# A hybrid decoder layer: how the plain weight tiles are split into high and low parts

## The chip, the cores and the metric

The kernel runs on one core of one Trainium2 chip. The metric is the device time of one execution in microseconds; of before there are three runs. The profile is of one execution of the same program, taken by the hardware profiler.

## The reference

One decoder layer works on 528 tokens (16 learned ones, then 512) of width 1024, float32:

```
h += 1/2 SwiGLU(rmsnorm(h))                 # 1024 -> 2 x 2816 -> 1024
u  = rmsnorm(h) @ w_in                      # q, k, v, forget gate, retention q, k, v, g, two gates
a  = forgetting attention, 16 heads of 64, causal, with a bias from the running log forget gate
b  = retention, 4 heads (128 -> 256), in chunks of 128, group norm, swish gate
h += (g_a * (a @ w_o_fox) + g_b * (b @ w_o_ret)) @ w_out
h += 1/2 SwiGLU(rmsnorm(h))
```

The result must agree with float32. So every float32 operand of a dense product is split: a high part that TensorE's float32r format holds exactly, and a low part, the operand less the high part. A product is three passes: high x high, high x low, low x high.

## The kernel before

Features lie on the 128 partitions, tokens on the free axis. A weight matrix is cut into *pieces* of 128 output features: 8 blocks of 128 x 128 beside each other (1024 columns), or for the output tiles of a SwiGLU 6 or 5 blocks (768 or 640 columns). The program takes the pieces in one fixed order, which is TensorE's own order, written out by hand; the list `SEQ` gives it for a SwiGLU. `n`, `a`, `b` are whole hidden tiles, `e` and `l` are hidden tiles made with seven products of quarters instead of eight, `p` is an output tile. After the first SwiGLU come the projections (`proj`, with the attention woven between them), the retention, three square products of eight output tiles each (`oa`, `ob`, `ow`), and the second SwiGLU. TensorE's instructions keep the program's order. For the other engines and the DMA queues a planner chooses the order: it takes what is ready by its own estimate of times, within the order of the program's priorities, so it also moves transfers ahead of older work once a buffer is free. Each queue then runs strictly in the order chosen.

There are two kinds of weight tiles. An *S* tile (kind `"S"`, 14 in each SwiGLU) serves an `e`/`l` pair; sums of its quarters are made by VectorE (`wsums`), and quarters and sums are split. All other tiles are *plain* (kind `"w"`). `load` brings a tile of 2048 columns (two pieces) on SP's queue into one of two float32 buffers (tag `w`); an S tile has two buffers of its own. `ready` makes the pieces `wh` and `wl` (tags of that name, four buffers each) by `split`: ScalarE copies the source into `wh`, VectorE subtracts `wh` from the source into `wl`. `weights()` hands TensorE's next piece over and calls `ready` for three pieces, that one and the next two. The first two pieces come from the tile `w0`, which is loaded in four quarters between the loads of the eight chunks of `h`; they are split in halves, alternating with `gained`, which makes the operands `n1uh` and `n1ul` from `h`. ScalarE and VectorE keep the program's order only in this first stage.

GpSimd's own work is small: constants at the start, some of which wait for the vector tile `VEC`; for each of 16 heads the load of a bias row `B` (line 760) and a sum `Bd` (line 761); the reloads of the gates `gs` (line 1034) and of `hh` (line 1091).

In the profile the copies into `wh` stand at line 105, the subtractions into `wl` at line 106, the tile loads at line 178, the matmuls of a whole piece at line 277. TensorE's groups are named by what they write: `fpa`, `fpb` (hidden tiles of the first SwiGLU), `fq` (its quarter products), `fpo` (its output tiles), `spa`, `spb`, `sq`, `spo` (the same of the second).

Of the kernel before, what the change touches and what calls it, by code (L numbers as in the profile page):

```python
"""Hybrid decoder layer (FoX attention + retention between two half SwiGLU blocks), one core.

Everything is kept feature-major: features on partitions, tokens on the free axis.  The zero rows
that the reference puts before the meta tokens are masked everywhere, so the token axis here has the
16 meta tokens followed by the 512 main ones.  Dense products split both float32 operands exactly
into a float32r high and low part and take three passes (hh, hl, lh).  Most hidden tiles of the
SwiGLU blocks are computed by seven products of quarters (output halves x contraction halves x token
halves) instead of eight; the sums of quarters are float32 sums, split exactly like the other operands.
"""
# [22 lines left out]
# The order of a SwiGLU's work on the tensor engine, one token a piece or two of weights:  n0, n1: the  # L32
# first two hidden tiles; aj, bj: the halves of hidden tile j; ej, lj: a hidden tile by seven products of
# quarters, its first four and its last three; pi: the next output tile of the i-th part of the hidden
# tiles.  ui marks where the i-th chunk's sums of quarters are made.
# [17 lines left out]
# Tensor engine work (in units of its time) put between the steps of the attention: FOXFILL scales it,  # L53
# CREDIT is the number of the gates' tiles that go with a pair of heads.
# [10 lines left out]
def layer(tc, order, hT, wf1i, wf1o, wf2i, wf2o, wmix, wsq, vecs, cs, rmask, rvec, cmask, outT):  # L65
# [3 lines left out]
    with ExitStack() as es:  # L69
# [24 lines left out]
        def po_(a):  # L94
            """Where token 0 lies in a two-bank PSUM tile: no matmul's tokens cross the banks."""
            return PO if a == 0 else PM
# [15 lines left out]
        def weave(main, fill):  # L112
            """Emit main; what it yields is the tensor engine time to fill before it goes on."""
            have = 0.0
            for need in main:
                have -= need
                while have < 0:
                    got = next(fill, None)
                    if got is None:
                        have = 0.0  # L120
                        break
                    have += got

        # ---------------------------------------------------------------- the weights' stream
# [43 lines left out]
        def load(n):  # L168
            while at["l"] < min(n, len(loads)):
                i = at["l"]  # L170
                src, w, kind = loads[i]
                if kind == "S":
                    if st["sp"] is None:
                        return
                    raw[i] = st["sp"].tile([128, 2048], F32, name=f"w{i}", tag="wS", bufs=2)
                else:
                    raw[i] = wp.tile([128, 2048], F32, name=f"w{i}", tag="w", bufs=2)
                ld = nc.sync.dma_start(raw[i][:, :w], src[:, :w])
                if i == 5:
                    with tc.issue_after(ld.ins):  # L180
                        nc.sync.dma_start(RV, rvec)
                at["l"] += 1

        def wsums(i):
            """Sums of a weight tile's quarters A11, A12, A21, A22: S1, S2, S4, and S3 in A21's place."""
# [9 lines left out]
        def ready(n):  # L195
            while at["p"] < min(n, len(pieces)):
# [7 lines left out]
                wh = wp.tile([128, 1024], F32R, name=f"wh{i}", tag="wh", bufs=4)  # L204
                wl = wp.tile([128, 1024], F32R, name=f"wl{i}", tag="wl", bufs=4)
                got[i] = wh, wl
                at["p"] += 1
                if i < 2:
                    for x in (0, 512):
                        split(wh[:, x:x + 512], wl[:, x:x + 512], raw[li][:, c + x:c + x + 512])  # L210
# [5 lines left out]
                else:  # L216
                    split(wh[:, :w], wl[:, :w], raw[li][:, c:c + w])

        def weights():
            i = at["u"]  # L220
            at["u"] += 1
            ready(i + 3)
# [3 lines left out]
        # ---------------------------------------------------------------- constants and first loads  # L226
# [4 lines left out]
        w0 = wp.tile([128, 2048], F32, name="w0", tag="w", bufs=2)  # L231
        raw[0] = w0
        at["l"] = 1
        for k in range(KC):
            if k < 4:
                nc.sync.dma_start(w0[:, 512 * k:512 * k + 512], wf1i[0][:, 512 * k:512 * k + 512])
# [7 lines left out]
        RV = cp.tile([128, 16], F32, name="RV")  # L244
        zeta, xi, xi2 = RV[:, 0:4], RV[:, 4:8], RV[:, 8:12]
# [22 lines left out]
        # ---------------------------------------------------------------- helpers  # L268
        def mm3(outs, w, x, nk, first=True, last=True):
            """outs = w^T x over nk chunks of 128, three float32r passes; outs: (psum, first token, end)."""  # L270
# [18 lines left out]
        def gained(k, g, u, a, name):  # L289
            """u = h * gain, split into high and low parts."""  # L290
# [14 lines left out]
        def rstd(acc, R, outs, a, name, er=None):  # L305
            """R = rsqrt(mean square + eps) of every token, on all partitions."""
# [16 lines left out]
        # ---------------------------------------------------------------- SwiGLU  # L323
# [4 lines left out]
        def usums(c, gain, a, xs, name):  # L328
            """Sums of the quarters of h * gain * R (chunk halves x token halves), split: they pair
            tokens, which have one scale only when they are normed."""  # L330
# [18 lines left out]
        def ffn(seq, u, gain, a, pst, pq, norm, done, name):  # L349
# [5 lines left out]
            def prod(out, w, off, x, k0, ts, first, last):  # L355
                """out (+)= w^T x over four chunks: one of the seven products of quarters."""
# [864 lines left out]
```

## Time and profile before

| | |
|---|---|
| runs, us | 1394.8 median, 1394.41 to 1395.88 |
| span of the profiled execution, us | 1392.1 |
| whole time of the profiled execution | not given on the page |
| instructions | 22206 |
| bytes moved by DMA | 139.41 MB |

The span runs from the first to the last instruction; what a run takes more lies around it. The page gives each engine's busy time, the chain of work that ended last, the waits with what ended them, and for DMA the share of the core's 16 DMA engines' time. PE is TensorE, ACT ScalarE, DVE VectorE, POOL GpSimd; SPq and POOLq are the queues on which SP and GpSimd issue transfers.

### The profile page before, as it was taken

The page shows a single profiled execution, that of the slowest core. Times are in us where ns is not written, and L with a number is a line of the kernel's source. Part 1 is how long each engine was busy: PE and PEld are TensorE (multiplying, and loading weights), DVE is VectorE, ACT ScalarE, POOL GpSimd, SP SyncE. Part 2 cuts the span into 40 slices and gives each one's busy share as a digit, 9 for nine tenths or more (in the row PEclk, how much of TensorE's full clock was granted, in tenths as well). Part 3 has the DMA queues.
Part 4 walks back from the last instruction along what each step waited for, and adds up shares of the span by engine and source line. Part 5 has one row for each costly group of instructions (what it writes and reads, how often), then busy time and mean ns, then how long its engine had stood idle before and what let it go on. Part 6 is the DMA issues. An engine that isn't in the chain of part 4 may idle for free.

```text
span 1392.1 us, 22206 instructions
## 1 busy us (share of the span) xinstructions
PE 1376.5 (99%) x8871; PEld 1232.8 (89%) x8871; DVE 1007.9 (72%) x1948; ACT 666.7 (48%) x1131; POOL 52.6 (4%) x80
## 2 busy tenths in 40 slices
PE   8999999999999999999999999999999999999999
PEld 7999999999988788877878998888888889899897
DVE  7977877866687676677755866754666977788773
ACT  7433333333567577666754534453435433344331
POOL 0000000000013000010000000000100000000000
PEclk9999999999999999999999999999999999999999
DMA  7123222221513222222222112433521232223302
GB/s 276 46 106 110 79 101 106 84 103 64 201 61 109 92 84 71 90 92 84 92 84 91 61 61 71 139 124 136 191 108 57 80 127 82 99 93 121 109 21 97
DMA packets 27814, 139.41 MB, mean 100 GB/s; under 512 B 3632, under 2 KB 4016, under 8 KB 16576
## 3 DMA queue, kind: packets, MB, share of 16 engines
q1 hardware_dynamic: 24336, 127.31, 25.5%
q0 software_dynamic: 3232, 10.65, 2.6%
q8 instruction: 70, 1.15, 0.3%
q14 instruction: 32, 0.26, 0.1%
q10 hardware_dynamic: 144, 0.04, 0.0%
HBM read 129.56 MB, written 8.42 MB: 99 GB/s over the span
## 4 chain that ended last, share of the span: by engine, by line
PE 96%; DVE 2%; ACT 1%; DMA 0%; issue 0%; SPq 0%; DVEq 0%; ACTq 0%
PE fq L287 10%; PE sq L287 10%; PE fpo L277 9%; PE spo L277 9%; PE pg L277 6%; PE prv L277 3%; PE fpb L277 3%; PE pq L277 3%; PE fpa L277 3%; PE pv L277 3%; PE ow L277 3%; PE spa L277 3%; PE ob L277 3%; PE spb L277 3%; PE prg L277 3%; PE oa L277 3%
## 5 line engine op out<-in xcount | busy, mean ns | idle before, releaser
L105 ACT ACTIVATE wh<-w 128x512 fp32r<-128x512 f32 (+3 forms) x299 | 249.7, 835 | 465.6 <-PE fpo L277 69.1
L106 DVE TENSOR_TENSOR wl<-w,wh 128x512 fp32r<-128x512 f32 (+3 forms) x299 | 282.9, 946 | 68.3 <-ACT wh L105 66.0
L277 PE MATMUL fpo<-fgh,wh 128*128 128x272 f32 x352 | 71.4, 284 | 0.0
L277 PE MATMUL fpo<-fgl,wh 128*128 128x272 f32 x352 | 71.4, 284 | 0.0
L277 PE MATMUL fpo<-fgh,wl 128*128 128x272 f32 x352 | 71.2, 284 | 0.0
L277 PE MATMUL spo<-sgh,wl 128*128 128x512 f32 (+1 forms) x181 | 70.1, 387 | 0.0
L277 PE MATMUL spo<-sgh,wh 128*128 128x512 f32 (+1 forms) x181 | 70.0, 386 | 0.0
L277 PE MATMUL spo<-sgl,wh 128*128 128x512 f32 (+1 forms) x181 | 69.9, 386 | 0.0
L106 DVE TENSOR_TENSOR pl<-PT,ph 128x512 fp32r<-128x512 f32 (+4 forms) x80 | 34.6, 434 | 32.7 <-ACT ph L105 31.5
L106 DVE TENSOR_TENSOR wl<-ws,wh 128x512 fp32r<-128x512 f32 x84 | 57.6, 686 | 0.0
L277 PE MATMUL pg<-n2uh,wh 128*128 128x512 f32 x128 | 56.4, 440 | 0.0
L1116 DVE SCALAR_TENSOR_TENSOR hh<-spo,hh 128x512 f32<-128x512 f32 (+1 forms) x33 | 22.3, 675 | 44.9 <-PE spo L277 44.9
L793 ACT ACTIVATE P<-P,st 128x144 f32<-128x144 f32 (+1 forms) x64 | 36.5, 570 | 36.9 <-DVE st L789 36.1
L277 PEld LDWEIGHTS fpo<-fgh,wl 128*128 128x128 f32 x352 | 54.1, 189 | 0.0
L277 PEld LDWEIGHTS fpo<-fgh,wh 128*128 128x128 f32 x352 | 54.0, 188 | 0.0
L277 PEld LDWEIGHTS fpo<-fgl,wh 128*128 128x128 f32 x352 | 54.0, 188 | 0.0
L105 ACT ACTIVATE wh<-ws 128x512 fp32r<-128x512 f32 x84 | 51.7, 616 | 0.0
L277 PE MATMUL pg<-n2uh,wl 128*128 128x512 f32 x128 | 50.6, 395 | 0.0
L277 PE MATMUL pg<-n2ul,wh 128*128 128x512 f32 x128 | 50.4, 394 | 0.0
L492 DVE SCALAR_TENSOR_TENSOR h<-fpo,h 128x528 f32<-128x528 f32 x32 | 22.6, 707 | 37.8 <-PE fpo L277 37.8
L287 PE MATMUL fq<-n1ul,wh 128*128 128x264 f32 x168 | 48.0, 285 | 0.0
L287 PE MATMUL fq<-n1uh,wh 128*128 128x264 f32 x168 | 47.9, 285 | 0.0
(926 smaller groups left out, 4296.4 us busy)
## 6 DMA issues: line engine op xcount, KB each, us to landing
w<-in_wmix SPq DMA_DIRECT2D x32, 1024.0 KB, 4.9
w<-in_wf2i SPq DMA_DIRECT2D x22, 1024.0 KB, 4.9
w<-in_wf1i SPq DMA_DIRECT2D x21, 1024.0 KB, 4.9
w<-in_wsq SPq DMA_DIRECT2D x12, 1024.0 KB, 4.9
w<-in_wf1o SPq DMA_DIRECT2D x8, 768.0 KB, 4.2
w<-in_wf2o SPq DMA_DIRECT2D x8, 768.0 KB, 4.2
w<-in_wf1o SPq DMA_DIRECT2D x8, 640.0 KB, 3.9
w<-in_wf2o SPq DMA_DIRECT2D x8, 640.0 KB, 3.9
```

What stands on the lines that cost most here:

```text
L105: nc.scalar.activation(xh, src, AF.Copy)
L106: nc.vector.tensor_tensor(xl, src, f32(xh), ALU.subtract)
L277: nc.tensor.matmul(out, p[:, o:o + 128], q[:, a:b], start=first and k == 0 and i == 0, stop=last and k == nk - 1 and i == 2)
L287: nc.tensor.matmul(out, p, q, start=start and i == 0, stop=stop and i == 2)
L492: nc.vector.scalar_tensor_tensor(h[m][:, x:y], ps, 0.5, h[m][:, x:y], ALU.mult, ALU.add)
L793: last["exp"] = nc.scalar.activation(P[i][:, :w], P[i][:, :w], AF.Exp, scale=-1.0, bias=st[:, 2:3], accum_out=sm[:, 0:1])
L1116: nc.vector.scalar_tensor_tensor(h[m][:, x:y], ps, 0.5, h[m][:, x:y], ALU.mult, ALU.add)
```

## The change

The plain tiles have no float32 copy in SBUF any more. Per piece GpSimd issues a transfer that casts the weight from HBM into `wh` (float32r); ScalarE writes minus `wh` into `wl`; and GpSimd issues a second transfer from HBM, which adds the weight to what stands in `wl`. `load` only notes the address of a plain tile. The two float32 buffers' space goes to `wh` and `wl`, six buffers each; `weights()` calls `ready` for five pieces. The first tile `w0` keeps its float32 form, in two buffers of the tag `wl`. The small load of `RV` is issued after the first loads. S tiles, sums, matmuls and their order stay. (The diff also takes out comments.)

```diff
@@ load @@
                 src, w, kind = loads[i]
-                if kind == "S":
-                    if st["sp"] is None:
-                        return
-                    raw[i] = st["sp"].tile([128, 2048], F32, name=f"w{i}", tag="wS", bufs=2)
-                else:
-                    raw[i] = wp.tile([128, 2048], F32, name=f"w{i}", tag="w", bufs=2)
-                ld = nc.sync.dma_start(raw[i][:, :w], src[:, :w])
-                if i == 5:
-                    with tc.issue_after(ld.ins):
-                        nc.sync.dma_start(RV, rvec)
                 at["l"] += 1
+                if kind == "w":
+                    raw[i] = src
+                    continue
+                if st["sp"] is None:
+                    at["l"] -= 1
+                    return
+                raw[i] = st["sp"].tile([128, 2048], F32, name=f"w{i}", tag="wS", bufs=2)
+                nc.sync.dma_start(raw[i], src)
@@ ready @@
-                wh = wp.tile([128, 1024], F32R, name=f"wh{i}", tag="wh", bufs=4)
-                wl = wp.tile([128, 1024], F32R, name=f"wl{i}", tag="wl", bufs=4)
+                wh = wp.tile([128, 1024], F32R, name=f"wh{i}", tag="wh", bufs=6)
+                wl = wp.tile([128, 1024], F32R, name=f"wl{i}", tag="wl", bufs=6)
...
                 if i < 2:
                     for x in (0, 512):
-                        split(wh[:, x:x + 512], wl[:, x:x + 512], raw[li][:, c + x:c + x + 512])
+                        split(wh[:, x:x + 512], wl[:, x:x + 512], raw[li][i][:, x:x + 512])
...
                 else:
-                    split(wh[:, :w], wl[:, :w], raw[li][:, c:c + w])
+
+                    nc.gpsimd.dma_start(wh[:, :w], raw[li][:, c:c + w])
+                    nc.scalar.activation(wl[:, :w], f32(wh[:, :w]), AF.Copy, scale=-1.0)
+                    nc.gpsimd.dma_start(wl[:, :w], raw[li][:, c:c + w], accum_op=ALU.add)
@@ weights @@
-            ready(i + 3)
+            ready(i + 5)
@@ first loads @@
-        w0 = wp.tile([128, 2048], F32, name="w0", tag="w", bufs=2)
+        w0 = [wp.tile([128, 1024], F32, name=f"w0{x}", tag="wl", bufs=6) for x in "ab"]
...
-                nc.sync.dma_start(w0[:, 512 * k:512 * k + 512], wf1i[0][:, 512 * k:512 * k + 512])
+                nc.sync.dma_start(w0[k // 2][:, 512 * (k % 2):512 * (k % 2) + 512], wf1i[0][:, 512 * k:512 * k + 512])
...
         RV = cp.tile([128, 16], F32, name="RV")
+        nc.sync.dma_start(RV, rvec)
```

## Rows read from the trace of the kernel before

**Rows 1.** The page's busy times: busy us, share of the span, instructions.

```profile
PE 1376.5 (99%) x8871; PEld 1232.8 (89%) x8871; DVE 1007.9 (72%) x1948; ACT 666.7 (48%) x1131; POOL 52.6 (4%) x80
```

**Rows 2.** Waits of TensorE: us in total, times, longest.

```profile
PE fpa L277 <- ACT n1uh L293: 6.1, 1, 6.1
...
PE PV L849 <- DVE pl L106: 1.3, 2, 0.9
```

**Rows 3.** Windows: length, busy us of PE, PEld, DVE, ACT, POOL; clock, DMA share, GB/s.

```profile
0.00:35.00 35.00, 28.75 (x216) 28.04 (x217) 25.91 (x36) 25.63 (x38) 2.11 (x14) 1.00 0.73 274
...
375.00:420.00 45.00, 42.69 (x298) 39.19 (x299) 32.26 (x53) 29.02 (x47) 5.32 (x5) 1.00 0.24 81
420.00:490.00 70.00, 67.51 (x356) 53.34 (x355) 51.23 (x142) 47.06 (x98) 14.63 (x13) 0.98 0.28 97
```

**Rows 4.** Groups by shape: xcount | busy us, mean ns | idle before, releasers.

```profile
L106 DVE TENSOR_TENSOR wl<-w,wh 128x1024 fp32r<-128x1024 f32 x119 | 146.5, 1231 | 39.8 <-ACT wh L105 38.5
...
L106 DVE TENSOR_TENSOR wl<-w,wh 128x768 fp32r<-128x768 f32 x32 | 30.6, 956 | 0.0
...
L106 DVE TENSOR_TENSOR wl<-w,wh 128x640 fp32r<-128x640 f32 x32 | 26.2, 820 | 8.2 <-ACT wh L105 8.2
L105 ACT ACTIVATE wh<-w 128x640 fp32r<-128x640 f32 x32 | 23.6, 737 | 56.9 <-PE spo L277 15.7 <-PE fpo L277 11.0 <-PE fq L287 7.1
```

**Rows 5.** DMA issues: xcount, KB each, median us from issue to landing.

```profile
w<-in_wmix SPq DMA_DIRECT2D x32, 1024.0 KB, 4.9
...
gs<-gsp POOLq DMA_DIRECT2D x16, 256.0 KB, 3.1
```

**Rows 6.** The weight tiles' loads of line 178.

```profile
DMA to landing us min/median/max: 3.6/4.8/12.3
```

**Rows 7.** The chain of waits, 370 to 500 us: start, us, what.

```profile
389.19 1.22 DVE wl L106
...
477.46 1.22 DVE wl L106
```

**Rows 8.** The page's DMA queues: packets, MB, share of 16 engines.

```profile
q1 hardware_dynamic: 24336, 127.31, 25.5%
q0 software_dynamic: 3232, 10.65, 2.6%
```

**Rows 9.** Window of the start, columns as in rows 3.

```profile
4.00:20.00 16.00, 13.74 (x95) 13.14 (x96) 13.37 (x19) 14.69 (x23) 1.09 (x5) 1.00 1.03 402
```

**Rows 10.** The chain of waits, 0 to 45 us.

```profile
2.58 5.01 DMA w<-in_wf1i
...
8.30 1.69 PE fpb L277 x6
...
20.38 5.81 PE fpa L277 x48
```

**Rows 11.** Timeline of the start: start, us, instruction, [idle before <-releaser].

```profile
4.79 0.24 POOL L260 TENSOR_SCALAR qg<-VEC 128x1 f32<-128x1 f32 x1 [3.19 <-DMA VEC<-in_vecs]
...
14.99 1.06 ACT L105 ACTIVATE wh<-w 128x1024 fp32r<-128x1024 f32 x1
```

**Rows 12.** The chain of waits over two runs of plain pieces.

```profile
345.39 29.13 PE fpo L277 x240
...
948.99 44.50 PE ob L277 x192
```

**Rows 13.** Windows of the same two runs, columns as in rows 3.

```profile
345.40:374.50 29.10, 29.10 (x240) 28.90 (x239) 22.54 (x30) 16.14 (x24) 0.00 (x0) 1.00 0.59 203
949.00:993.50 44.50, 44.50 (x193) 36.09 (x193) 26.33 (x34) 19.95 (x27) 9.59 (x18) 1.00 0.55 189
```

**Rows 14.** Timeline of GpSimd in the attention.

```profile
430.36 1.28 POOL L761 TENSOR_TENSOR Bd<-B,CM 128x512 f32<-128x512 f32 x1 [2.93 <-DMA B<-negc]
431.59 0.55 POOL L760 DMA_DIRECT2D B<-negc  x1
```

## The prediction

> **What bounds the kernel now.** I read the busy times first. TensorE is busy 1376.5 of 1392.1 us, VectorE 1007.9 [rows 1]. So a lighter VectorE buys nothing by itself: all that any change of the weights' preparation can win lies in the 15.6 us in which TensorE is idle. The waits by engine and the windows say where these are. The largest is 6.1 us before the first matmul [rows 2], and the first 35 us hold 28.75 us of TensorE work; 2.31 and 2.49 us are lost between 375 and 490 us, where the attention starts [rows 3]; the remaining 4.5 us lie elsewhere, most of them behind the last matmul. The view of TensorE's waits has nine rows; the second, 1.3 us in two waits, is the longest after the start, and none names a weight tile [rows 2]. So weights are ready early today, and the change can lose far more than it can win.
>
> **The change part by part.** *Plain pieces.* By shape there are 119 pieces of 1024 columns, 32 of 768 and 32 of 640, 183 in all. VectorE's subtractions for them go: 146.5 + 30.6 + 26.2 = 203.3 us. ScalarE keeps one copy of the same shape per piece, now the negation of wh, 1.06 us at 1024 columns [rows 11] and 0.74 at 640 [rows 4]: no change. GpSimd gets 2 x 183 = 366 transfers; it took 0.55 us to issue a plain one [rows 14], so about 201 us. All of this is beside TensorE, and as busy time costs 0.
>
> *What the lighter VectorE is worth.* Four of the removed subtractions stand on the chain of waits between 385 and 480 us, the first and the last of 1.22 us and 4.7 us in all [rows 7]; TensorE's idle time there is 4.8 us [rows 3]. ScalarE's copies stay, and now each needs a transfer that has landed. I take half of what VectorE gave: -2 us, between 0 and -4.7.
>
> *Bytes.* The plain pieces are 119 x 0.524 + 32 x 0.393 + 32 x 0.328 = 85.5 MB. They leave SP's queue, which took 25.5% for 127.31 MB (2.79 us per MB of all 16 engines), and enter GpSimd's, which took 2.6% for 10.65 MB (3.40 us per MB) [rows 8], twice. Share of the transfer engines: 25.5 - 17.1 + 2.6 + 2 x 20.9 = 53%. No row shows a casting or an accumulating transfer; from below I price both as GpSimd's plain ones. From above no row limits them; the slowest landing of a weight load, 12.3 us against a median of 4.8 [rows 6], is between two and three times the usual, so I let 12.3 us stand for the upper end of a single transfer.
>
> *The start.* From 4 to 20 us the transfer engines are full: share 1.03 at 402 GB/s [rows 9]. TensorE's steady run hangs on the third quarter of the first weight tile, issued at 2.58 and 5.01 us under way; the first matmul of the second half starts at 8.30, right behind its split [rows 10]. Before, everything else was behind this on the same SP queue. Now the casting transfers of pieces 2 to 5 (4 x 0.52 = 2.1 MB) need nothing but free buffers, and GpSimd idles 3.19 us until VEC lands at 4.79 [rows 11]. Started early they run beside the loads of w0 and h, at half rate each: what SP moved between 3.5 and 7.6 us takes up to 4 us longer. Started after VEC they cost about 1. I take +2 (0 to 4). The chunks of h that follow come no faster than TensorE uses them then (0.27 MB at 200 GB/s is 1.4 us; the 12 matmuls of a chunk in two pieces take 12 x 5.81 / 48 = 1.45 us [rows 10]), so the shift stays.
>
> Then the low part of piece 2. ScalarE's copy began at 14.99 [rows 11], VectorE's subtraction followed. Now ScalarE's negation ends at 16.05, GpSimd issues, and the transfer lands 3.1 us (GpSimd's 256 KB [rows 5]) to 12.3 us later, while the engines are still full. TensorE wants it two matmuls into the run that begins at 20.38 [rows 10], at 20.9: early by 1.7, late by up to 8. I take 6 us for the landing, 22.4, so +1.5. Piece 3 has its own 5.9 us run of cover after that and I cost it at 0. Start in all: +3.5, between 0 and +12.
>
> *The steady state.* Six buffers instead of four let a piece start five ahead. For a 1024-column piece the path is cast 4.0 us (between 256 KB at 3.1 and 1024 KB at 4.9 [rows 5]) + negation 1.06 + issue 0.55 + accumulation 4.0 = 9.6 us, and five pieces of 44.50 / 8 = 5.56 us give 27.8 [rows 12]. So latency is covered threefold. The new wait is another matter: the accumulating issue stands in GpSimd's queue until ScalarE has negated, and whatever is queued behind it (the next cast, the biases B, the gates gs, the reloads hh) stands too. Where each accumulation is queued ahead of the next cast, a piece takes GpSimd 4.0 + 1.06 + 0.55 = 5.6 us, just TensorE's 5.56. GpSimd's own rows show this habit: 2.93 us of waiting for a B load, the Bd sum, then the next B load [rows 14]. In the run of eight output tiles at the end of the first SwiGLU the pitch is 29.13 / 8 = 3.64 us and such a piece takes 3.3 + 0.74 + 0.55 = 4.6, eight times 0.95 late = 7.6 us, against a lead of 5 x 3.64 - 7.9 = 10.3 us. So at these prices little shows. With ScalarE's own queue in the way I take +3 for all runs, between 0 (casts run ahead) and what rival 1 gives.
>
> **The sum.** 1392.1 + 3.5 - 2 + 3 = 1396.6 in the profiled execution's span. The page gives no other time of that execution; the runs' median is 1394.8, 2.7 us more, for what lies around the span. So 1399.3; I say 1399, and 1395 to 1405 for this case.
>
> **Rivals.** *1. GpSimd's queue becomes the bound.* Cast, wait, accumulate in series, with a cast that lands in 4.9 us and half a microsecond before ScalarE comes to it, is 7.0 us a piece. The 24 pieces of the three square products and the first 10 of the second SwiGLU then lose 34 x 1.44 = 49 us, less a lead of 18 us: +31; the attention, where 16 Bd sums hold GpSimd another 4 us each [rows 14], adds 0 to 40. For it: GpSimd waits behind its own loads today [rows 14]. Against: the waits there are no longer than one load, and the planner can put the next cast ahead. About +40: 1435; with a cast at twice the price, up to 1490.
>
> *2. The accumulation takes the transfer engines twice as long.* Share 53 + 21 = 74% over the whole, but not evenly. In the run of the ob products it is 0.55 today, at the end of the first SwiGLU 0.59 [rows 13]. There 4.2 MB, dearer by 0.61 us each for the cast and then 2 x 3.40 us each for the accumulation, are 31 us of 44.5: 1.25, 11 us late against a lead of 18. At the SwiGLU's end about 3.5 MB so priced bring 1.48, 14 us late against 10.3: +4. With the start's accumulations later by another 3 to 5 us: 1407 (1403 to 1415). The Trainium skill speaks for it: its page "Collectives: The Full Stack", section "The bandwidth ceiling: the fold count and why AG ≠ RS ≠ AR", says that an adding transfer costs no time for the add but reads two sources, which halves its rate. No run here shows it; by that page the forecast would be 1407, by GpSimd's plain row 1399.
>
> *3. Faster.* If the casts are issued behind VEC and the first accumulation lands in time, the start costs 0, the dense runs hold, and the whole chain at the attention's start shortens by VectorE's 4.7 us: 1390 to 1391. For it: the four subtractions on the chain. Against: ScalarE's copies stand on the same chain and get a transfer ahead of them. It decides at a start below 1 us.
>
> *4. Hidden throughout:* start and relief cancel, 1394.8 within 2.8.
>
> *5. A wall:* an accumulation of four times the plain price is 53 + 3 x 20.9 = 116% of the transfer engines: 1600 and more.
>
> **Chances.** Forecast 0.30, rival 1 0.23, rival 2 0.14, rival 3 0.13, rival 4 0.13, rival 5 0.07. What a measurement can tell from no change is about 0.2%, 2.8 us. Faster by more: 0.13, all of rival 3. Within: rival 4 and the part of the forecast below 1397.6, 0.13 + 0.10 = 0.23. Slower: 0.64. The range 1391 to 1465 leaves out part of rival 3 (0.06), the upper quarter of rival 1 (0.06) and the wall (0.07).
>
> **What would show it.** The start: piece 2's matmuls wait for a transfer named wl at about 22 us, and the first of fpb starts between 9 and 12 us instead of 8.30. The relief: the gaps at 390 and 434 us shrink by about a microsecond each. Rival 1: matmuls of ob, ow, spa wait for wl while GpSimd waits for ScalarE's wl, and the transfer share there stays well below 1. Rival 2: the same waits with the share at 1. The sum is wrong if TensorE waits for weights in the interleaved middle of a SwiGLU, where I cost it at nothing, or if the start's first matmul stays at 8.30.

## The result and the profile after

The changed kernel takes 1623.1 us (median of four runs, 1622.4 to 1624.0) against 1394.6 for the kernel before on the same chip: a ratio of 1.164, 95% interval 1.162 to 1.166. That is far above the predicted 1399 and above the range's end of 1465. The profiled execution's span is 1620.6 us, 228.5 more than before.

The busy times of the page, as in [rows 1]:

```profile
PE 1450.5 (90%) x8871; PEld 1278.8 (79%) x8871; DVE 811.6 (50%) x1765; ACT 652.8 (40%) x1131; POOL 312.1 (19%) x446
```

VectorE is lighter by 196 us (203 worked out). TensorE does the same 8871 matmuls and is idle for 170.1 us instead of 15.6, which is +154. It is also *busy* for 74 us longer. The two make up the 228.

The waits of all engines in the kernel after (engine, line, waited for: us in total, times, longest):

```profile
POOL wl L218 <- ACT wl L217: 658.6, 131, 9.8
ACT wl L217 <- DMA wh<-in_wmix: 200.8, 54, 8.1
ACT wl L217 <- DMA wh<-in_wf1o: 119.3, 21, 10.9
...
ACT wl L217 <- DMA wh<-in_wf2o: 91.8, 20, 11.8
...
ACT wl L217 <- DMA wh<-in_wsq: 75.5, 15, 8.7
ACT wl L217 <- DMA wh<-in_wf2i: 62.0, 13, 8.2
```

Line 217 is the negation, line 218 the accumulating transfer. GpSimd stands 658.6 us before accumulations because the negation has not been made; ScalarE stands about 550 us before negations because the cast has not landed (the five rows' sum is 549.4). Neither wait is in the trace of before.

TensorE's own waits, the answer to [rows 2]:

```profile
PE PV L849 <- ACT ph L105: 23.6, 15, 3.9
PE fpo L279 <- DVE h L494: 14.0, 4, 4.1
PE PV L848 <- DVE pl L106: 13.6, 8, 2.8
PE r1vt L957 <- DVE r1v L106: 13.1, 1, 13.1
...
PE ow L279 <- ACT mh L105: 9.0, 3, 6.2
...
PE spb L279 <- DMA wl<-in_wf2i: 3.6, 3, 1.6
```

Hardly any of these names a weight. TensorE waits for the *other* products of ScalarE and VectorE: attention's `ph` and `pl`, the retention's `r1v`, the mix `mh`, `h`. For `mh` the timelines below show that it is late because it stands behind a negation in ScalarE's queue; that the others are late for the same reason is borne out by e1_const below, where these waits are gone or under 1 us. The windows by stage show where (length, busy us of PE, PEld, DVE, ACT, POOL; granted clock, DMA share, GB/s); first the kernel before, then the one after, attention with retention, the three square products, and the second SwiGLU:

```profile
375.40:896.60 521.20, 516.69 (x3126) 439.55 (x3127) 369.88 (x861) 311.89 (x595) 38.35 (x39) 1.00 0.25 85
896.60:1038.00 141.40, 140.90 (x637) 114.64 (x637) 77.60 (x114) 62.64 (x90) 11.19 (x21) 1.00 0.41 144
```

```profile
426.00:1054.00 628.00, 552.05 (x3122) 461.46 (x3123) 286.63 (x792) 303.93 (x591) 128.20 (x169) 0.94 0.55 124
1054.00:1224.00 170.00, 149.55 (x642) 118.06 (x642) 50.21 (x92) 62.48 (x90) 44.05 (x66) 0.95 0.75 186
1224.00:1620.00 396.00, 363.56 (x2105) 317.14 (x2103) 226.19 (x429) 131.12 (x207) 63.95 (x89) 0.96 0.55 132
```

Over these stages the transfer engines are at 55 to 75%, not at 100. The clock column falls from 1.00 to about 0.95, and TensorE's busy time rises with it (516.7 to 552.1 us for the attention's matmuls).

One place shows the whole mechanism: the start of `ow`. Timelines of the kernel after (start, us, instruction, [idle before <- what ended it]) of GpSimd, VectorE, ScalarE and TensorE, and then five windows of the same stretch, columns as above:

```profile
1172.73 0.88 POOL L218 DMA_DIRECT2D wl<-in_wsq  x1 [2.66 <-ACT wl L217]
1173.27 0.90 POOL L216 DMA_DIRECT2D wh<-in_wsq  x1
1181.70 0.87 POOL L218 DMA_DIRECT2D wl<-in_wsq  x1 [7.53 <-ACT wl L217]
1182.26 0.87 POOL L216 DMA_DIRECT2D wh<-in_wsq  x1
```

```profile
1175.55 0.69 DVE L1082 TENSOR_TENSOR gs<-gs,gs 128x512 f32<-128x512 f32 x1
```

```profile
1173.56 0.63 ACT L105 ACTIVATE mh<-gs 128x512 fp32r<-128x512 f32 x1 [1.14 <-DVE gs L1082]
1180.35 1.06 ACT L217 ACTIVATE wl<-wh 128x1024 fp32r<-128x1024 f32 x1 [6.16 <-DMA wh<-in_wsq]
1181.32 0.61 ACT L105 ACTIVATE mh<-gs 128x512 fp32r<-128x512 f32 x1
```

```profile
1181.98 0.80 PE L279 MATMUL ow<-mh,wh 128*128 128x512 f32 x1 [6.25 <-ACT mh L105]
1182.71 0.80 PE L279 MATMUL ow<-ml,wh 128*128 128x512 f32 x1
```

```profile
1172.00:1178.00 6.00, 2.02 (x6) 0.78 (x5) 3.48 (x6) 1.06 (x2) 1.45 (x2) 0.79 0.93 169
1178.00:1184.00 6.00, 2.02 (x4) 1.39 (x5) 0.69 (x1) 1.57 (x2) 2.30 (x5) 0.50 0.33 87
1184.00:1190.00 6.00, 6.00 (x23) 4.77 (x23) 0.00 (x0) 1.06 (x1) 3.43 (x7) 0.85 0.98 234
...
1174.00:1176.00 2.00, 1.25 (x3) 0.48 (x3) 1.74 (x3) 0.19 (x1) 0.18 (x1) 0.88 0.91 131
1176.00:1178.00 2.00, 0.00 (x0) 0.00 (x0) 0.24 (x1) 0.00 (x0) 0.00 (x0) 0.50 1.01 221
```

GpSimd issues a cast at 1173.27, behind the accumulation of an earlier piece. ScalarE reaches the negation of a cast that has not landed, and stands for 6.16 us. `mh`, whose input was ready (VectorE had written `gs` by 1176.24), waits behind it. TensorE waits 6.25 us for `mh`. GpSimd waits too, 7.53 us before the accumulation, and only behind that comes the next cast at 1182.26. So the loop is closed: cast, landing, negation, accumulation, next cast. It takes 8.97 us from one accumulation to the next (1172.73 to 1181.70): 0.54 to the start of the cast, 7.08 from there to the negation, 1.06 of negation, and 0.29 until the accumulation starts. TensorE needs 5.56 us a piece [rows 12].

When TensorE starts again, its matmul takes 0.80 us instead of the usual 0.39 to 0.40: the granted clock is 0.50, the lower level of 1.2 GHz. It had fallen as the long wait began (0.88 from 1174 to 1176, 0.50 from 1176 on), after two groups of three matmuls with waits of 1.45 and 1.25 us before them.

The transfer engines were full for part of this stretch (0.93 in the first window), so the place by itself does not tell late transfers from the loop. The squares before it do. Windows of `oa` and `ob` in the kernel after:

```profile
1054.50:1121.30 66.80, 56.06 (x253) 44.39 (x252) 19.27 (x45) 26.04 (x41) 11.70 (x17) 0.95 0.68 174
1121.30:1166.40 45.10, 44.80 (x194) 35.92 (x192) 13.27 (x20) 16.38 (x22) 14.97 (x23) 1.00 0.80 198
```

In `oa` the accumulations come one by one, 8.3 to 9.2 us apart from 1078.67 to 1122.68, and the product takes 66.8 us instead of 52.2. In `ob` there is sometimes a second cast ahead of an accumulation, the accumulations come in part in pairs (1122.68 and 1124.12, 1142.52 and 1145.59), and the product takes 45.1 us instead of 44.5, at a higher transfer share than `oa`.

### The profile page after: what moved, and what is told of

Its sections match the earlier page's. It is cut to its first block, busy times and chain, and to the rows that moved or that the text cites. A ratio compares the mean times of both kernels' runs of the same rounds, so it can differ in the third digit from the quotient of the medians.

```text
span 1620.6 us, 22600 instructions
## 1 busy us (share of the span) xinstructions
PE 1450.5 (90%) x8871; PEld 1278.8 (79%) x8871; DVE 811.6 (50%) x1765; ACT 652.8 (40%) x1131; POOL 312.1 (19%) x446
## 3 DMA queue, kind: packets, MB, share of 16 engines
q0 software_dynamic: 55936, 181.59, 50.7%
## 5 line engine op out<-in xcount | busy, mean ns | idle before, releaser
L217 ACT ACTIVATE wl<-wh 128x1024 fp32r<-128x1024 f32 (+2 forms) x183 | 176.1, 964 | 643.6 <-DMA wh<-in_wmix 200.8
L218 POOL DMA_DIRECT2D wl<-in_wmix x65 | 57.4, 883 | 321.9 <-ACT wl L217 231.4
L105 ACT ACTIVATE wh<-w 128x512 fp32r<-128x512 f32 x112 | 69.3, 622 | 89.5 <-PE fq L289 19.3
L106 DVE TENSOR_TENSOR wl<-w,wh 128x512 fp32r<-128x512 f32 x112 | 76.8, 686 | 51.6 <-ACT wh L105 51.5
L279 PE MATMUL fpo<-fgh,wh 128*128 128x272 f32 x352 | 75.3, 297 | 21.7 <-DVE h L494 14.0
L279 PE MATMUL spo<-sgh,wh 128*128 128x512 f32 (+1 forms) x181 | 72.6, 401 | 12.2 <-DVE hh L1118 6.7
L279 PE MATMUL fpo<-fgl,wh 128*128 128x272 f32 x352 | 74.9, 295 | 0.1
L216 POOL DMA_DIRECT2D wh<-in_wmix x65 | 48.2, 747 | 67.3 <-PE pv L279 29.4
L218 POOL DMA_DIRECT2D wl<-in_wf1o x32 | 29.0, 917 | 120.4 <-ACT wl L217 111.5
L279 PEld LDWEIGHTS spo<-sgh,wh 128*128 128x128 f32 x181 | 35.4, 195 | 20.9 <-DVE hh L1118 7.6
L218 POOL DMA_DIRECT2D wl<-in_wf2o x32 | 28.6, 893 | 117.3 <-ACT wl L217 111.7
```

The costliest lines, as they stand in the source:

```text
L105: nc.scalar.activation(xh, src, AF.Copy)
L106: nc.vector.tensor_tensor(xl, src, f32(xh), ALU.subtract)
L216: nc.gpsimd.dma_start(wh[:, :w], raw[li][:, c:c + w])
L217: nc.scalar.activation(wl[:, :w], f32(wh[:, :w]), AF.Copy, scale=-1.0)
L218: nc.gpsimd.dma_start(wl[:, :w], raw[li][:, c:c + w], accum_op=ALU.add)
L279: nc.tensor.matmul(out, p[:, o:o + 128], q[:, a:b], start=first and k == 0 and i == 0, stop=last and k == nk - 1 and i == 2)
```

## The experiments

Three theories. **A**, the closed loop: ScalarE's queue keeps its order, so it waits for a cast, and GpSimd's next cast stands behind the accumulation that waits for ScalarE; each wait lengthens the other. **B**, the transfers: accumulations are dear, casts land late, and that is enough by itself. **C**, GpSimd: the number of its issues is the bound, whatever their order. The expectations of e1_const, e2_noacc, e3_castahead and e4_sub use words of their own: their loop theory is A, their transfer theory is B taken as the price of the transfers alone, and their queue theory is none of these three; it says that only GpSimd's blocked queue costs time, and ScalarE's own standing does not. All kernels but the changed one, e8_hybrid and e10_middle ran once; a kernel run once is compared with the kernel before on the same chip (1394.8 for e1_const, e2_noacc, e3_castahead and e4_sub, 1394.1 for e3b_ahead, e5_actwait, e6_negpool and e7_late, 1394.6 for e9_late3, 1394.3 for e11_twocasts). The planner orders the queues of every kernel afresh, so each run differs from its neighbour in other places of the queues too.

The stages in us, from the first matmul of one to that of the next (`pff`, `oa`, `spa`), for all kernels:

```
                first SwiGLU  attention+retention  squares  second SwiGLU    span
before                 375.4                521.2    141.4          354.1  1392.1
after                  425.8                628.7    169.2          396.9  1620.6
e1_const               383.8                517.3    140.9          353.7  1395.7
e2_noacc               379.7                540.8    142.7          353.7  1416.9
e3_castahead           486.6                555.8    146.8          463.5  1652.7
e4_sub                 383.6                558.5    147.8          358.1  1448.0
e5_actwait             395.9                537.3    148.4          355.7  1437.3
e3b_ahead              394.1                560.3    146.2          375.6  1476.2
e6_negpool             437.2                549.0    192.5          420.9  1599.6
e7_late                449.7                517.5    141.2          429.4  1537.8
e8_hybrid              377.7                518.8    149.0          353.9  1399.4
e9_late3               392.8                517.3    140.9          366.4  1417.4
e10_middle             376.0                518.2    141.8          354.5  1390.5
e11_twocasts           382.8                518.0    140.9          353.7  1395.4
```

**1. e1_const: the negation reads a constant instead of `wh`.**

```diff
-  nc.scalar.activation(wl[:, :w], f32(wh[:, :w]), AF.Copy, scale=-1.0)
+  nc.scalar.activation(wl[:, :w].rearrange("p (a b) -> p a b", b=128),
+                       onesD.unsqueeze(1).to_broadcast([128, w // 128, 128]), AF.Copy, scale=-1.0)
```

> ScalarE fills wl from a constant tile instead of from minus wh, so nothing waits for a cast but TensorE; casts, accumulations, their bytes and ScalarE's instructions stay (the low parts are the whole weight less a constant: that part of the result is left wrong). Loop theory (ScalarE's in-order queue waits for each cast to land, GpSimd's next cast stands behind an accumulation that waits for ScalarE): the wait goes, 1396 to 1410 us. Transfer theory (casting and accumulating transfers are too dear for the 16 engines): 1550 us or more, the transfer share stays near 0.6 with TensorE waiting for wh and wl. Queue theory (only GpSimd's blocked queue matters): the same as the loop theory here.

Measured: 1397.5 us. ScalarE's, GpSimd's and the transfers' work is all there (312 us of GpSimd, 181.59 MB), and 225 of the 228 us are gone. What is taken away is that ScalarE's instruction waits for the cast to land. That rules out C, and of B the part by which the price of the transfers would cost time. The queue theory forecast the same here as A.

**2. e2_noacc: no accumulating transfer**; `wl` is left at minus `wh`.

```diff
-  nc.gpsimd.dma_start(wl[:, :w], raw[li][:, c:c + w], accum_op=ALU.add)
```

> The accumulating transfer is left out (wl stays minus wh), cast and negation stay. So GpSimd's queue never waits for ScalarE, and 85.5 MB less are moved; ScalarE still stands in line for each cast to land. Loop theory: part of the loss stays, since ScalarE still waits where the planner put the negation, but casts are now issued as soon as a buffer is free: 1400 to 1450 us. Queue theory: back to 1395 to 1400. Transfer theory: about half of the loss, 1480 to 1520.

Measured: 1418.7 us, as A expected and above the 1400 of the queue theory. GpSimd's queue holds no accumulation any more, so the loop is open; ScalarE still waits for casts, which land in 4.1 us (median of the projections' and the squares'). The rest, +24, lies nearly all in the attention (540.8 against 517.3 in e1_const). So ScalarE's wait by itself, without the loop and without the accumulations' bytes, costs a tenth of the loss.

**3. e3_castahead and 4. e3b_ahead: GpSimd's queue is told to put accumulation i behind cast i+2.** e3b_ahead drops that order where an S piece stands in between.

```diff
+  cast = nc.gpsimd.dma_start(wh[:, :w], raw[li][:, c:c + w])
+  low(i - 2, cast)      # negation of piece i-2; its accumulation issued behind this cast
+  pend.append((i, wh, wl, raw[li][:, c:c + w], w))
```

> The whole calculation, but each accumulation is put behind the cast of a piece two further on in GpSimd's queue, and the negation is emitted there. Loop theory: up to three casts are under way at once, so the period of about 8.7 us a piece falls below TensorE's 5.6; what stays is ScalarE's waiting for casts at the planner's places: 1410 to 1480 us. Queue theory: 1395 to 1405. Transfer theory: no change, 1600 or more.

> The full calculation; accumulation i is issued right behind cast i+2 where the two pieces in between are plain, and without such an order where an S piece follows (in e3_castahead the order also held across S pieces). Negation on ScalarE as in the change. Theory A: casts run ahead of the accumulations in the dense stages, the loop of 8.5 to 9 us a piece is opened there and ScalarE's wait shortens, 1430 to 1500, with the SwiGLUs still late. Theory B: the casts still land in over 6 us and ScalarE waits as long, 1570 to 1630. Theory C (the number of GpSimd's issues is the bound, whatever their order): 1600 and more.

Measured: 1654.5 and 1478.0 us. The first lies outside A's range and, by the number alone, in the transfer theory's. Its stages say otherwise: the dense stages came down to 555.8 and 146.8 us, but the SwiGLUs went up to 486.6 and 463.5: where S pieces lie between, the next plain cast needs a buffer that frees much later, and the accumulation now waits for that cast. TensorE's waits there, of e3_castahead, do name the weights:

```profile
PE spo L292 <- DMA wl<-in_wf2o: 42.8, 13, 6.0
PE fpo L292 <- DMA wl<-in_wf1o: 41.3, 12, 5.9
```

So the first was more a test of the order that I had set than of the theory. The second keeps the gain in the dense stages (560.3, 146.2) and loses less in the SwiGLUs than the changed kernel. Only places in the queues separate it from the changed kernel: 145 us less with the same transfers. That is in A's range, below those of C and B.

**5. e4_sub: no negation and no accumulation.** SP brings the float32 piece into a buffer of its own and VectorE subtracts; the cast stays; four buffers each, and three pieces ahead.

```diff
+  wf = wp.tile([128, 1024], F32, name=f"wf{i}", tag="wf", bufs=4)
+  nc.sync.dma_start(wf[:, :w], raw[li][:, c:c + w])
+  nc.vector.tensor_tensor(wl[:, :w], wf[:, :w], f32(wh[:, :w]), ALU.subtract)
```

> The cast stays, but the low part is made as before: the float32 piece comes on SP's queue into a buffer of its own (four of each kind, three pieces ahead) and VectorE subtracts wh from it. No accumulation, no negation; ScalarE has 176 us less, VectorE its 203 us back, the bytes are those of the change. Loop theory: no queue waits for ScalarE, and the waiting for the cast moves to VectorE, whose queue it holds where the planner is too early: 1395 to 1440. Transfer theory: 1550 or more if the cast is the dear one, about 1400 if the accumulation is. Queue theory: 1392 to 1397.

Measured: 1449.8 us, 10 above the upper end of what A gave. The wait has moved to VectorE's queue, and attention pays again (558.5). Its largest row:

```profile
DVE wl L219 <- DMA wh<-in_wmix: 77.6, 39, 7.9
```

So it isn't peculiar to ScalarE or to the accumulation: an in-order engine with other work that waits for a cast is enough for a loss of this order (55 us here, 24 in e2_noacc). How much of the 55 comes from the shorter lead and the fewer buffers was not taken apart.

**6. e5_actwait: ScalarE waits for every cast, but the accumulation doesn't.** VectorE fills `wl` from a constant; ScalarE reads one column of `wh`.

```diff
-  nc.scalar.activation(wl[:, :w], f32(wh[:, :w]), AF.Copy, scale=-1.0)
+  nc.vector.tensor_copy(wl[:, :w].rearrange("p (a b) -> p a b", b=128),
+                        onesD.unsqueeze(1).to_broadcast([128, w // 128, 128]))
+  nc.scalar.activation(lk, f32(wh[:, 0:1]), AF.Copy, scale=-1.0)
```

> All transfers at full bytes, but wl is filled by VectorE from a constant tile instead of with -wh, so the accumulating transfer no longer waits for the cast; ScalarE instead reads one column of each wh that has landed, so its queue still waits for every cast. (The low parts are left wrong.) It separates the two halves of the wait. Theory A (closed loop: ScalarE waits for the cast, GpSimd's next cast stands behind the accumulation that waits for ScalarE; the loop multiplies the wait): without the loop only ScalarE's wait for a landing of 4 to 5 us is left, like the run without the accumulation (1418.7): 1405 to 1440. Theory B (the accumulations slow the casts' landing, and ScalarE's wait for it in order is enough by itself): ScalarE still waits some 500 us, 1550 to 1630.

Measured: 1439.1 us, at A's upper end; B wanted 1550 and more. ScalarE still waits for nearly as long in total,

```profile
L219 ACT ACTIVATE lk<-wh 128x1 f32<-128x1 f32 x183 | 36.8, 201 | 535.7 <-DMA wh<-in_wmix 155.0
```

535.7 us idle before the 183 small reads (busy, mean ns, idle before), all of it ended by a cast's landing, against 568.6 us in the changed kernel (the rows above and 19.3 for `in_wf1i`). The accumulations' bytes are in flight, and yet 184 us of the loss are gone. This row is the best lesson of the study: nearly the same total of an engine's waiting is worth 42 us (1437.3 against e1_const's 1395.7) when it is not part of a loop, and 225 when it is. Two things go with it: the total is spread over 163 waits here and 130 there, and ScalarE is busy for 130 us less (522.9), VectorE for 108 more.

**7. e6_negpool: GpSimd makes the negation itself**, with the order of e3b_ahead.

```diff
-  nc.scalar.activation(wl[:, :w], f32(wh[:, :w]), AF.Copy, scale=-1.0)
+  nc.gpsimd.tensor_scalar_mul(wl[:, :w], f32(wh[:, :w]), -1.0)
```

> The same order of GpSimd's queue as e3b_ahead, but GpSimd makes the negation itself: ScalarE and VectorE never wait for a transfer of a plain piece. Theory A: attention's and the SwiGLUs' work on ScalarE and VectorE is on time again; GpSimd needs per 1024-column piece 0.55 + 0.9 of issue and 1 to 2 us of negation, below TensorE's 5.56, so 1395 to 1440, if the cast is two ahead. Theory C (GpSimd's queue is the bound): TensorE waits for wl itself in the dense runs, 1480 or more, and no wait of ScalarE names wh.

Measured: 1601.3 us, which A had not expected. The timeline of GpSimd in the square products says why:

```profile
1068.48 2.77 POOL L198 TENSOR_SCALAR wl<-wh 128x1024 fp32r<-128x1024 f32 x1 [4.00 <-DMA wh<-in_wsq]
1071.20 0.59 POOL L229 DMA_DIRECT2D wh<-in_wsq  x1
1071.79 0.93 POOL L203 DMA_DIRECT2D wl<-in_wsq  x1
1076.72 2.76 POOL L198 TENSOR_SCALAR wl<-wh 128x1024 fp32r<-128x1024 f32 x1 [4.00 <-PE ob L293]
```

The negation takes 2.77 us there, each stands right behind the transfers of the piece before, and GpSimd waits 4.0 us before it, the first of the two shown for a cast to land: 8.24 us a piece, in series. Now TensorE does wait for the weights themselves (`ob` 12.2 us in 7 waits, `oa` 11.8 in 5, all `<- DMA wl<-in_wsq`). This is the series of the prediction's rival 1 with the negation on GpSimd, and with the sign on TensorE that it named.

**8. e7_late and 9. e9_late3: the full calculation, with the negation held back.** Casts stay five pieces ahead. The negation and its accumulation are issued two pieces (e9_late3: three) before use, behind the last matmul traced so far, so that the cast has landed when ScalarE comes to it.

```diff
-  nc.scalar.activation(wl[:, :w], f32(wh[:, :w]), AF.Copy, scale=-1.0)
-  nc.gpsimd.dma_start(wl[:, :w], raw[li][:, c:c + w], accum_op=ALU.add)
+  pend.append((i, wh, wl, raw[li][:, c:c + w], w))
@@ weights @@
   ready(i + 5)
+  low(i + 2)            # e9_late3: low(i + 3); makes both, behind the last matmul
```

> The full calculation with ScalarE's negation; the cast of a piece stays five pieces ahead, but its negation and its accumulation are put about two to three pieces before use, behind the last matmul traced so far, so that a cast has some three pieces (10 to 16 us) to land before ScalarE comes to it. Theory A: ScalarE's wait is gone and the loop with it, 1393 to 1410. Theory B: landing of 6.6 us is covered too, so the same time, but the accumulations collide with the casts in the runs of plain pieces, 1400 to 1430. Theory C: GpSimd's queue carries as many issues as before, 1580 or more.

> e7_late with the negation and accumulation one piece earlier (three pieces before use instead of two). In e7_late the SwiGLUs lost 74 and 75 us and TensorE waited there for wl to land, 11.9 us in four waits between 90 and 200 us. Theory A' (the accumulation's landing of 7 us is not covered by two output-tile pieces of 3.64 us): the SwiGLUs come back to within 10 us each of before, 1400 to 1425. Rival (in the SwiGLUs it is the order on ScalarE and GpSimd again, S pieces' splits and casts behind a held negation): still over 1480. Dense stages: unchanged by A', since two pitches of 5.56 us still cover the cast.

Measured: 1539.6 and 1419.2 us. In the dense stages the question between A and B is settled: with the whole change in place, attention and squares take 517.5 and 141.2 us, *less* than before. Windows of these two stages in e7_late, columns as above:

```profile
449.70:967.20 517.50, 515.62 (x3126) 438.06 (x3127) 293.20 (x797) 309.21 (x594) 128.62 (x169) 1.00 0.69 153
967.20:1108.40 141.20, 141.17 (x636) 114.45 (x636) 49.62 (x89) 62.81 (x89) 45.29 (x68) 1.00 0.93 232
```

In the squares the transfer engines are at 0.93 and TensorE loses 0.03 us. In the SwiGLUs two pieces were too short a lead, and the expectation for e7_late missed it: an output-tile piece takes 3.64 us, an accumulation lands in 5.7 to 7.4 (medians of the output tiles), and TensorE waited for `wl` (100.3 us in all, 57.5 of it in `fpo` and `spo`). With three pieces that is cured for the most part: +17.4 and +12.3 us remain, of which 5.0 are there when `fpo` starts (88.9 against 83.9). So 204 of the 228 us of the loss were a matter of *when* the same instructions stand in their queues.

**10. e8_hybrid and 11. e10_middle: the change where it pays.** The kernel before, with casts and held-back negations only for the projections and the squares (e10_middle: without the first four pieces of the projections and the eight of `ow`), in the four buffers that are there.

```diff
-  feed(wmix[i], [1024] * min(2, NMIX - 2 * i))
-  feed(wsq[i], [1024, 1024])
+  feed(wmix[i], [1024] * min(2, NMIX - 2 * i), "c" if i >= 2 else "w")   # e8_hybrid: "c"
+  feed(wsq[i], [1024, 1024], "c" if i < 8 else "w")                      # e8_hybrid: "c"
@@ ready @@
+  elif loads[li][2] == "c":      # cast now; low() negates and accumulates two pieces before use
```

> The kernel before with the change made only for the pieces of the projections and of the three square products (89 of 183): cast by GpSimd three pieces ahead into the four wh buffers, negation on ScalarE and accumulation two pieces ahead, behind the last matmul traced so far; the SwiGLUs keep SP's loads and VectorE's subtractions. In e7_late these two stages took 517.5 and 141.2 us against 521.2 and 141.4 before, so theory A (with the wait out of ScalarE's queue, what is left of the change is the lighter VectorE): 1394.2 - 3.9 = 1390 to 1391, if three pieces of 5.56 us cover 4.7 us of cast, 1.1 of negation, 0.9 of issue and 7.0 of accumulation. Theory B (with one piece less of lead than e7_late the transfers' landing is not covered): TensorE waits for wl in the square products, 1400 to 1430.

> e8_hybrid with the change made only in the middle: the first four pieces of the projections and the eight pieces of ow are split as before, since e8_hybrid lost 6.6 us in ow (44.5 to 51.1 between its first matmul and that of spa, where the loads for the second SwiGLU run too) and 2.3 us up to the first matmul of pff. Theory A (the rest of the change is a lighter VectorE, worth 2.4 to 3.9 us in the attention): 1390.5 to 1392.5, just to be told from the kernel before. Rival (the loss at both ends comes with the step between the two kinds of weights, wherever it stands): 1396 to 1402.

Measured: e8_hybrid 1401.9 us, ratio 1.006 (1.004 to 1.007), above A's 1391 and where its expectation had the theory of too short a lead; e10_middle 1392.3 us (11 runs) against 1394.3 (15 runs), ratio 0.9987 (0.9978 to 0.9996). e8_hybrid lost 7.6 us in the squares: TensorE waited 4.5 us in `ow` for `wl`, where GpSimd also issues eight reloads of `hh`, seven of them in one stretch of 4.09 us. Without `ow` and the first pieces that loss is gone and the attention keeps 3.0 us. It is 2.0 us or 0.13% below the kernel before, and the interval only just leaves out no change. More was not to be had: in the attention stage TensorE was idle for 4.5 us before.

**12. e11_twocasts: e1_const with a second casting transfer in place of the accumulating one.**

```diff
-  nc.gpsimd.dma_start(wl[:, :w], raw[li][:, c:c + w], accum_op=ALU.add)
+  nc.gpsimd.dma_start(wl[:, :w], raw[li][:, c:c + w])
```

> e1_const with the accumulating transfer replaced by a second casting transfer of the same bytes (the low parts are left wrong): it prices the accumulation by itself. If an accumulation costs the transfer engines what a plain transfer of GpSimd's costs, GpSimd's queue shows the same share as in e1_const, 58.9%; by the price worked out from the difference of e1_const and e2_noacc (5.8 us per MB against 3.4), 58.9 - 85.5 x 2.4 / 1396 = 44%, and the second transfer lands in some 4.6 us instead of 7.5. Time by every theory 1393 to 1398.

Measured: 1397.2 us, as e1_const. GpSimd's queue (packets, MB, share of 16 engines) and its transfers (KB each, median us to landing) in e1_const, then in e11_twocasts:

```profile
q0 software_dynamic: 55936, 181.59, 58.9%
...
wh<-in_wmix POOLq DMA_DIRECT2D x65, 512.0 KB, 4.9
wl<-in_wmix POOLq DMA_DIRECT2D x65, 512.0 KB, 7.3
```

```profile
q0 software_dynamic: 55936, 181.59, 43.8%
...
wh<-in_wmix POOLq DMA_DIRECT2D x65, 512.0 KB, 4.2
wl<-in_wmix POOLq DMA_DIRECT2D x65, 512.0 KB, 4.9
```

The same bytes cost 611 us of the queue's share as casts (0.438 x 1395.4, 3.37 us per MB) and 822 with 85.5 MB of them accumulated: an accumulated MB costs 3.37 + 211 / 85.5 = 5.83 us, 1.73 times a cast one. Between these two single runs the time moves by 0.3 us.

## Why the prediction was wrong, point by point

**The step that failed** is the steady state: "At these prices little shows. With ScalarE's own queue in the way I take +3 for all runs, between 0 (casts run ahead) and what rival 1 gives." Measured, the changed kernel's +228.5 less the start's 13.1 and plus the relief's 3.9 is +219. The cycle of cast, negation and accumulation was priced at 4.0 + 1.06 + 0.55 = 5.6 us; at the start of `ow` it takes 8.97, and in `oa` 8.3 to 9.2. The mis-sized term is the cast: 7.0 us from issue to landing (median, `wh` of the squares; 6.6 in the projections), not 4.0. The accumulations are what makes it late: without them, in e2_noacc, it is 4.1, and with casts in their place, in e11_twocasts, 4.6 and 4.2; with them, but with nothing that waits for a cast, in e1_const, 5.8 in the squares and 4.9 in the projections. In the changed kernel's projections the 33 casts that start within 0.7 us behind an accumulation land in 7.0 and the other 32 in 5.3. The issue was priced rightly: an accumulation's row is 0.88 us long, but the next instruction starts 0.54 behind its start. A cycle of 5.6 was close enough to TensorE's 5.56 that a term off by three microseconds turned "covered threefold" into a stream slower than its reader wherever one cast at a time is under way. That five pieces of lead did not help is no surprise then: a lead covers latency, and this was the rate.

**"ScalarE keeps one copy per piece: no change ... costs 0"** was the same error in the change's first part. The instruction's busy time is the same (652.8 us against 666.7), but it now waits for a transfer, and the prediction named what is queued behind the accumulation on GpSimd and not what is queued behind the negation on ScalarE. That is attention's `ph`, the SwiGLUs' `fgh`, `h` through VectorE, and `mh`. Outside any loop it costs 24 us without accumulations (e2_noacc) and 42 with them (e5_actwait).

**Rival 1** had the right mechanism, the wrong place and too small a price. It had the cycle in series at 7.0 us and 1435, up to 1490, and expected TensorE to wait for `wl`. Its sign "GpSimd waits for ScalarE's `wl`, and the transfer share stays well below 1" came true (658.6 us; 0.55 to 0.75); its sign on TensorE did not: there the waits named `ph`, `h`, `mh`. I had priced the stages by how late the weights are, and the largest part of the loss, 107.5 of 228.5 us, came in the attention, where ScalarE's *other* work is needed soonest; rival 1 had 0 to 40 there. It also left out the first SwiGLU, which lost 50.4.

**A term that was not in the sum at all** is TensorE's clock. The kernel before, busy 99% of the time, shows a mean clock of 1.00 over each of the four stages; in the kernel after the stages' means are 0.94 to 0.96, and single stretches have 0.50, as at 1178 us above. That goes with the 74 us of added busy time, a third of the loss: the 1376.5 us of before, divided by the mean clock of 0.948, are 1452, and 1450.5 were measured. In e7_late's dense stages, where TensorE has hardly any gaps, the clock is 1.00 again and the busy time 515.6 us.

**The start** was sized at +3.5, between 0 and +12, for the first 35 us. The first matmul of `fpb` starts at 8.8 us instead of 8.3, which is below the 9 to 12 that was named as the sign. The other sign came: TensorE waits 2.9 us for `wl` and goes on at 26.1. The first matmul of `fpo` comes 13.1 us later than before in the changed kernel (97.0 against 83.9); up to there TensorE is idle for 12.8 us instead of 6.3 and busy for 84.2 instead of 77.6, at a mean clock of 0.95, so half of the delay is the clock again. It is 2.7 late in e2_noacc (I had 2 for the casts), 8.4 in e1_const and 7.5 in e11_twocasts, which has casts in the accumulations' place: a second transfer per piece, of either kind, makes it late by some 5 us more (I had 1.5), in a stretch where the transfer engines are full (1.00 from 20 to 40 us in the changed kernel). The casts were issued behind `VEC`, at 6.04 us, as rival 3 assumed, and it did not help enough. The first accumulation was issued at 20.37, not at 16.05: its negation came behind other work of ScalarE and ended at 20.06.

**The relief** was right in kind and a little small: -2 of at most -4.7. The attention stage is 3.9, 3.7 and 3.9 us shorter in e1_const, e7_late and e9_late3. In e1_const 2.6 us of this are idle time of TensorE that is gone (1.88 left of 4.51), as the sign at the attention's start had it, and the rest is busy time.

**Rival 2**, the dear accumulation, was nearly right about the price, 1.73 times a cast's engine time, and wrong about its worth: it adds nothing to the total where nothing waits for a cast (e1_const against e11_twocasts). Where something does wait, the landing times above say that it costs by making the casts late. The Trainium skill's page "Collectives: The Full Stack", section "The bandwidth ceiling: the fold count and why AG ≠ RS ≠ AR", explains a ReduceScatter at half an AllGather's rate by the second source that the add reads. It says this of rings of several ranks; for one core's accumulating transfers the traces give 1.73, not 2. Rivals 3 and 4 failed with the forecast; rival 5 (four times the price) is excluded by the 1.73.

**The sign of a wrong sum**, TensorE waiting for weights in the interleaved middle of a SwiGLU, came only weakly in the changed kernel (3.6 us for `wl` in `spb`) and fully in e3_castahead and e7_late, whose accumulations come later.

**Still open**: how the loss divides between waiting and the slow clock that the waiting brought. By count it is 33.5 us idle and 16.9 busy in the first SwiGLU, 71.4 and 36.1 in the attention, 20.0 and 7.9 in the squares, 29.6 and 13.2 in the second SwiGLU; but a slower TensorE also changes when buffers come free, and no run held the one and changed the other.

## What to carry to other kernels

When a copy is turned into an instruction that waits for a transfer, its busy time says nothing: list what stands behind it on its engine, and look for a way back from that engine to the issue of the next transfer, since such a loop runs at the sum of its latencies (8.97 us here). Six buffers instead of four did not keep it from forming; no run changed their number alone. Price the loop with landing times under the load that it makes itself, not with the idle ones. The repair is to place the waiting instruction where its transfer has landed anyway; here that gave back 204 of 228 us with every instruction kept.

## What the runs showed of the hardware that was not expected

- A casting transfer costs what GpSimd's plain ones cost (3.37 us per MB against 3.40 before [rows 8]) and lands for 512 KB in 4.0 to 4.6 us where there are no accumulations (medians by weight matrix, e2_noacc), in 4.9 to 7.2 where there are (e1_const). An accumulating one costs 5.83 us per MB and lands in 7.3 to 7.7 (e1_const). Its row on GpSimd is 0.88 us long against 0.55, but the next instruction starts 0.54 us after it in either case.
- GpSimd takes 2.77 us for a negation of 128 x 1024 (e6_negpool) that ScalarE does in 1.06.
- With the granted clock at 0.50, matmuls of 512 columns took 0.80 us instead of 0.40; in the changed kernel's `ow` it fell as a wait of 6.25 us began, after two groups of three matmuls with waits of 1.45 and 1.25 us before them.
